# Output projection, LayerNorm and routing of three of four tiles moved into the mixers of a two-layer decoder trunk

## The chip, the core and the metric

One core of a Trainium2 chip runs the whole kernel. Its engines are PE (TensorE, matrix products; PEld is its weight load), DVE (VectorE), ACT (ScalarE), POOL (GpSimd) and SP (SyncE, which issues most transfers). The metric is the time of one execution on the device in microseconds (us). Each engine works through its own queue in order; an instruction that waits holds up all that stands behind it on its engine.

## The reference, cut to what matters

Two layers over 512 positions of 1024 features in float32, 16 experts of width 512, two of which a position uses.

```python
for l in range(2):
    mix = even_mixer(...) if l % 2 == 0 else odd_mixer(...)       # attention, ends in "@ w_o[l]"
    x = layer_norm(ALPHA * x + mix, ln_g[l, 0], ln_b[l, 0])       # LN1
    ffn = routed_moe(x, router_w, router_b, w_gate[l], w_up[l], w_down[l])
    x = layer_norm(ALPHA * x + ffn, ln_g[l, 1], ln_b[l, 1])       # LN2
...
def routed_moe(x, router_w, router_b, ...):
    aff = sigmoid(x @ router_w); sel = aff + router_b
    # best group of 4 experts by the sum of its two best; then the two best experts in it
    # gates: the two aff of the chosen experts, divided by their sum
    for e in range(16):
        h = silu(x @ w_gate[e]) * (x @ w_up[e])
        y = y + gates[:, e:e + 1] * (h @ w_down[e])
```

## The kernel before

The 512 positions are four tiles of 128. Every weight chunk of 1 MB (128 x 2048) is split on the core into a high part (ACT's cast `wh`, L184) and a low part (`wl`, L185, mostly on DVE, some on Pool), and every product is three matmuls (L197 wh by high, L198 wl by high, L199 wh by low). A tile scheduler orders the instructions of each engine; the strings `EVEN_ORDER`, `ODD_ORDER` and `ROUTE_ORDER` give the order in which the program offers the stages to it.

A mixer ends in attention over query tiles: a0 to a3 in layer 0 (span 0 to about 206 us), c0 to c3 in layer 1 (602 to about 820). One such tile is scores (L322, L323), maximum and bias on DVE (L342), exponential on ACT (L356), a multiplication by the reciprocal (`p`, L364, DVE or Pool), transposes (L372), ACT's copies `pT` (L375) and value matmuls (L378), and a split of the result into `XH` and `XL`. `o0` and `o1` are out_proj0, the half of the output projection that needs only the other mixer's heads. When all tiles are done, `out_proj` follows: for each tile `tile_y` (24 projection matmuls, the add into `xr` with L569, bn_stats L570, transposes L574, copy `yT` L576 and logits L578) and `tile_ln` (rsqrt in eight small DVE steps, the logits `u` L584 and L585, ACT's Sigmoid L586 and Identity L587, and the affine by `lnt`: L254 multiplies, L255 adds; `LN1_DVE` says how many of the 1024 columns DVE takes, the rest is Pool's). Then `choose` (L416 to L452) picks the experts of some tiles, `slots` gives each chosen row a slot of the first expert in a one-hot `oh` (L477), and `first_rows` multiplies by it to collect expert 0's rows in PSUM (L488).

`moe` runs the 16 experts: gate and up products (`ps_s`), silu times up, down product (`ps_a`), about 17.7 us an expert. Expert 0's rows come from first_rows, split into `m`; those of the others from an indirect gather (L1089, Pool) of the copy `x1d` in memory, by the index `idx` that `after_slots` makes with eight one-hot matmuls on `R` (L504); a second set of eight (L526, on `og`) gives the gates by slot. `AHEAD` lists the first sixteen chunks in the order in which SP is to load them; each waits for the buffer that it goes into. At the end of a layer, LN2 runs tile by tile: add with a running sum on DVE (L1228), Square on ACT (L1236), Pool and DVE sharing the rest (L1246 to L1256), while layer 1's first weights, the latents' (128 x 968 chunks), are split on Pool.

## Time and profile before

| | us |
|---|---|
| median of 3 runs (1188.57 to 1193.22) | 1191.38 |
| the profiled execution | 1197.56 |
| its span in the trace | 1195.7 |
| PE busy | 1098.3 (92%) |
| DVE, ACT, POOL busy | 935.3, 763.3, 263.2 |

The profile shows one execution, so sums made from its rows are set against 1197.56 and not against the median. Starts are in us from the start of the span. Matmuls overlap, so the time of one in a row (0.39 for a 128x512 matmul) is longer than the distance to the next; the distance is the pace.

### The profile page before, as it was taken

What the parts mean: (1) busy time and instruction counts of PE and PEld (TensorE: products, weight loads), DVE (VectorE), ACT (ScalarE), POOL (GpSimd) and SP (SyncE); (2) the same over time, 40 slices, a digit from 0 to 9 for tenths busy, and PEclk for the clock granted to TensorE, in tenths of its full rate; (3) what the DMA queues carried; (4) which work ended last, traced back from release to release, by engine and by line L of the source; (5) the groups of instructions that cost most, each with busy time, mean ns of one, the idle gap of its engine ahead of it and who ended that gap; (6) DMA issues with size and microseconds to landing.
All of it is one profiled execution on the core that took longest, in us unless ns stands there. A gap on an engine that the chain in (4) does not pass through costs nothing.

```text
span 1195.7 us, 16655 instructions
## 1 busy us (share of the span) xinstructions
PE 1098.3 (92%) x5739; PEld 816.4 (68%) x5739; DVE 935.3 (78%) x1866; ACT 763.3 (64%) x1229; POOL 263.2 (22%) x223
## 2 busy tenths in 40 slices
PE   6999999979999999997599889999799999999972
PEld 5886777867777777776277665777677777777751
DVE  3646746597999999995866999865879999999957
ACT  3557556225888888885435744754268888888852
POOL 2001240251111141102612133003411112311023
PEclk9999999988999999998699999999789999999986
DMA  8313423679899997996512211335699999989952
GB/s 206 116 36 78 83 55 141 246 278 309 295 362 348 353 334 252 365 370 218 163 27 71 71 36 36 106 106 194 247 292 288 368 338 354 329 263 369 370 193 107
DMA packets 139613, 262.25 MB, mean 219 GB/s; under 512 B 11831, under 2 KB 28247, under 8 KB 139520
## 3 DMA queue, kind: packets, MB, share of 16 engines
q1 hardware_dynamic: 129232, 234.62, 57.1%
...
q8 instruction: 47, 0.77, 0.3%
q14 instruction: 46, 0.38, 0.1%
...
## 4 chain that ended last, share of the span: by engine, by line
PE 80%; DVE 10%; ACT 5%; issue 2%; POOL 2%; DMA 1%; SPq 0%; DVEq 0%; ACTq 0%; POOLq 0%
PE ps_a L198 11%; PE ps_a L199 11%; PE ps_a L197 11%; PE ps_s L197 10%; PE ps_s L198 10%; PE ps_s L199 9%; PE ps_o L378 4%; PE ps_t L372 3%; DVE wl L185 2%; ACT wh L184 2%; PE ps_t L1100 2%; PE ps_s L322 1%; POOL wl L185 1%; PE ps_s L323 1%; PE ps_s L578 1%
## 5 line engine op out<-in xcount | busy, mean ns | idle before, releaser
L185 DVE TENSOR_TENSOR wl<-wraw,wh 128x1024 fp32r<-128x1024 f32 (+1 forms) x418 | 500.2, 1222 | 92.8 <-ACT wh L184 82.2
L184 ACT CAST wh<-wraw 128x1024 fp32r<-128x1024 f32 (+3 forms) x436 | 445.8, 1039 | 151.3 <-PE ps_s L199 67.0
L197 PE MATMUL ps_s<-wh,m 128*96 128x512 f32 (+1 forms) x528 | 209.2, 396 | 1.7 <-ACT m L202 1.7
L198 PE MATMUL ps_s<-wl,m 128*96 128x512 f32 (+1 forms) x528 | 206.9, 392 | 0.0
L199 PE MATMUL ps_s<-wh,m 128*96 128x512 f32 (+1 forms) x528 | 205.7, 389 | 0.4 <-DVE m L203 0.4
L198 PE MATMUL ps_a<-wl,hH 128*96 128x512 f32 x256 | 102.4, 400 | 10.4 <-POOL wl L185 10.4
L199 PEld LDWEIGHTS ps_s<-wh,m 128*96 128x96 f32 x528 | 86.7, 164 | 35.8 <-DVE m L203 1.3
L197 PEld LDWEIGHTS ps_s<-wh,m 128*96 128x96 f32 x528 | 87.2, 165 | 34.9 <-ACT m L202 2.1
L198 PEld LDWEIGHTS ps_s<-wl,m 128*96 128x96 f32 x528 | 86.9, 165 | 32.1 <-issue 0.2
L197 PE MATMUL ps_a<-wh,hH 128*96 128x512 f32 x256 | 103.1, 403 | 3.4 <-ACT hH L202 3.4
L199 PE MATMUL ps_a<-wh,hL 128*96 128x512 f32 x256 | 101.4, 396 | 1.3 <-DVE hL L203 1.3
L197 PE MATMUL ps_a<-wh,XH 128*128 128x512 f32 (+2 forms) x224 | 88.6, 395 | 2.6 <-ACT wh L184 1.5
L1089 POOL DMA_INDIRECT m<-x1d,idx x30 | 32.6, 1087 | 257.5 <-PE ps_t L1100 218.6
L199 PE MATMUL ps_a<-wh,XL 128*128 128x512 f32 (+2 forms) x224 | 88.1, 393 | 0.4 <-DVE XL L203 0.4
L1164 POOL DMA_INDIRECT yd<-m,idx x30 | 48.6, 1621 | 179.4 <-ACT m L1163 178.7
L198 PE MATMUL ps_a<-wl,XH 128*128 128x512 f32 (+2 forms) x224 | 87.5, 391 | 0.0
L197 PE MATMUL ps_a<-XH,wh 128*128 128x512 f32 x160 | 65.1, 407 | 0.0
L199 PE MATMUL ps_a<-XH,wl 128*128 128x512 f32 x160 | 64.7, 404 | 0.3 <-DVE wl L185 0.3
L198 PE MATMUL ps_a<-XL,wh 128*128 128x512 f32 x160 | 64.9, 406 | 0.0
L375 ACT COPY pT<-ps_t 128x512 f32<-128x512 f32 (+2 forms) x88 | 43.6, 518 | 31.8 <-PE ps_t L372 28.3
L356 ACT ACTIVATE p<-p,nm 128x256 f32<-128x256 f32 (+3 forms) x96 | 50.7, 530 | 18.4 <-DVE nm L349 9.3
L198 PEld LDWEIGHTS ps_a<-wl,hH 128*96 128x96 f32 x256 | 41.7, 163 | 27.0 <-POOL wl L185 11.8
...
## 6 DMA issues: line engine op xcount, KB each, us to landing
...
```

The source lines that it names most:

```text
L184: first(A.copy(hv, w))
L185: first(eng.tensor_tensor(out=lv, in0=w, in1=hv.bitcast(F32), op=ALU.subtract))
L197: T.matmul(o, lh, rh, start=first, stop=False)
L198: T.matmul(o, lh, rl, start=False, stop=False)
L199: T.matmul(o, ll, rh, start=False, stop=last)
L356: A.activation(out=pt[h], in_=(pt if bias else Sp)[h], func=AF.Exp, bias=nm[:, h:h + 1], scale=(slopes[0][h] if slopes else 1.0), accum_ou ...
L372: T.transpose(tp[h][:, j * 128:(j + 1) * 128], pt[h][:, j * 128:(j + 1) * 128], ident)
L375: A.copy(d_, s_)
L378: T.matmul(O[h * 64:(h + 1) * 64, c0:c0 + 128], vcols(j, h), pT[h][:, j * 128:(j + 1) * 128], start=(j == 0), stop=(j == nb - 1))
L1089: G.indirect_dma_start(out=xg_of[e], out_offset=None, in_=x1d[:, :], in_offset=bass.IndirectOffsetOnAxis(ap=idx[:CAP, e:e + 1], axis=0), b ...
L1100: T.transpose(p[:, k * CAP:(k + 1) * CAP], xg[:, (c * 4 + k) * 128:(c * 4 + k + 1) * 128], ident[:CAP, :CAP])
L1164: G.indirect_dma_start(out=yd[:, :], out_offset=bass.IndirectOffsetOnAxis(ap=idx[:CAP, e:e + 1], axis=0), in_=yos[e % 2], in_offset=None, ...
```

## The change

The output projection's second half, LN1 and the choice of tiles 0 to 2 are now stages inside the mixers' order strings (class `OutProj`: `S` loads, `y` projects and normalizes a tile, `x` applies the affine and writes the tile out, `h2` chooses for tiles 0 and 1). Tile 2's choice and affine and all of tile 3 stand in `all_routed`, behind the mixer. The mean comes from a sum taken with the add, the variance from ACT's Square instead of bn_stats; the logits are copied out of PSUM. The affine of tiles 2 and 3 is DVE's for all 1024 columns, that of tiles 0 and 1 Pool's as before. `R` now holds index and gate side by side in float32, so eight one-hot matmuls replace two sets of eight. The splits of the first two gate chunks and of expert 0's rows are kept in program order behind the one-hot of tile 3 (`issue_after(oh.ins)`). What only the end needs (`oht`, the flag) is made in expert 4. The value matmuls take the second head first. Chunk 7 is loaded last of the sixteen, into another buffer. Both halves of the latents' weights are loaded early instead of one.

```diff
-AHEAD = (2, 3, 4, 0, 1, 5, 6, 8, 9, 10, 12, 13, 7, 14, 11, 15)
-LN1_DVE = (0, 0, 0, 256)
+AHEAD = (2, 3, 4, 0, 1, 5, 6, 8, 9, 10, 12, 13, 14, 11, 15, 7)
+LN1_DVE = (0, 0, 1024, 1024)
-EVEN_ORDER = "a0 a1 a2 a3 o0 o1"
-ODD_ORDER = "d0 q0 d1 q1 R0 d2 d3 r0 r1 t1 t2 t3 c0 c1 o0 o1 c2 c3"
-ROUTE_ORDER = "y0 l0 y1 l1 y2 l2 y3 l3 r02 r23 r34"
+EVEN_ORDER = "a0 o0 a1 o1 S0 y0 x0 a2 y1 x1 h2 a3 y2"
+ODD_ORDER = "d0 q0 d1 q1 R0 d2 d3 r0 r1 t1 t2 t3 c0 c1 o0 o1 S0 c2 y0 x0 y1 x1 h2 c3 y2"
...
         for j in range(nb):
-            for h in range(2):
+            for h in (1, 0):
...
-        R = sm.tile([128, NT * 2, NE], F16, name="R", bufs=1)
-        V.tensor_tensor(out=R, in0=Of, in1=recc.rearrange("p t c -> p (t c)").unsqueeze(2).to_broadcast([128, 8, NE]), op=ALU.mult)
+        R = sm.tile([128, NT * 2, 2, NE], F32, name="R", bufs=1)
+        V.tensor_tensor(out=R[:, :, 0, :], in0=Of, in1=recc.rearrange("p t c -> p (t c)").unsqueeze(2).to_broadcast([128, 8, NE]),
+                        op=ALU.mult)
+        weights()
+        V.tensor_tensor(out=R[:, :, 1, :], in0=Of, in1=gates.rearrange("p t c -> p (t c)").unsqueeze(2).to_broadcast([128, 8, NE]),
+                        op=ALU.mult)
         sp = ps_s()
         for j in range(NT * 2):
-            oh = sm.tile([128, CAP], F16, name="oh", bufs=4)
-            V.tensor_scalar(oh, slot1, pos[:, j:j + 1], None, op0=ALU.is_equal)
-            T.matmul(sp[:CAP, 0:NE], oh, R[:, j, :], start=(j == 0), stop=(j == NT * 2 - 1))
+            eq = sm.tile([128, CAP], F32, name="eq")
+            V.tensor_scalar(eq, slot1, pos[:, j:j + 1], None, op0=ALU.is_equal)
+            T.matmul(sp[:CAP, 0:2 * NE], eq, R[:, j].rearrange("p c e -> p (c e)"), start=(j == 0), stop=(j == NT * 2 - 1))
         V.tensor_scalar(idx[:CAP], sp[:CAP, 0:NE], OOB, None, op0=ALU.add)
+        A.activation(out=gslot[:CAP], in_=sp[:CAP, NE:2 * NE], func=AF.Copy, scale=1.0 / ALPHA)
...
-        sg = ps_t()
-        for j in range(NT * 2):
-            eq = sm.tile([128, CAP], F32, name="eq")
-            V.tensor_scalar(eq, slot1, pos[:, j:j + 1], None, op0=ALU.is_equal)
-            T.matmul(sg[:CAP, 0:NE], eq, og[:, j, :], start=(j == 0), stop=(j == NT * 2 - 1))
-        A.activation(out=gslot[:CAP], in_=sg[:CAP, 0:NE], func=AF.Copy, scale=1.0 / ALPHA)
...
+        def y(self, i, room):
             for c in range(2):
                 ys = xr[i][:, c * 512:(c + 1) * 512]
-                V.tensor_tensor(out=ys, in0=ys, in1=half_proj(rows[c], oH, oL, g, i), op=ALU.add)
-                V.bn_stats(sts[i][:, c, :], ys)
-                if main:
+                V.tensor_tensor_reduce(out=ys, in0=half_proj(self.rows[c], self.oH, self.oL, self.g, i), in1=ys, scale=1.0,
+                                       scalar=(self.ls[:, i, 0:1] if c else 0.0), op0=ALU.add, op1=ALU.add,
+                                       accum_out=self.ls[:, i, c:c + 1])
-                    yT = work.tile([128, 512], F32, name="yT", tag="sg", bufs=2)
+                    yT = room()
                     A.copy(yT, p)
                     for k in range(4):
-                        T.matmul(lgs[:, c, i, :], yT[:, k * 128:(k + 1) * 128], rwg[:, c * 4 + k, :],
+                        T.matmul(p[:, 0:NE], yT[:, k * 128:(k + 1) * 128], self.rwg[:, c * 4 + k, :],
                                  start=(k == 0), stop=(k == 3))
+                    V.tensor_copy(self.lg[:, i, c, :], p[:, 0:NE])
+        def ln(self, i, room):
+            ls = self.ls[:, i]
+            V.tensor_scalar(ls[:, 2:3], ls[:, 1:2], -1.0 / (D * 32), None, op0=ALU.mult)
+            sq = room().bitcast(BF16)
+            A.activation(out=sq, in_=xr[i], func=AF.Square, bias=ls[:, 2:3], scale=1.0 / 32, accum_out=ls[:, 4:5])
+            rs = rsqrt(ls[:, 4:5], LN_EPS, 1)
+            nm = sm.tile([128, 1], F32, name="nmr", bufs=4)
+            V.scalar_tensor_tensor(out=nm, in0=ls[:, 2:3], scalar=32.0, in1=rs, op0=ALU.mult, op1=ALU.mult)
+            A.activation(out=xr[i], in_=xr[i], func=AF.Identity, scale=rs, bias=nm)
+        def x1(self, i):
+            affine(xr[i], self.gb, self.bb, LN1_DVE[i])
...
+        room = lambda: work.tile([128, 512], F32, name="yT", tag="sg", bufs=2)
+        n = NT - 1
+        out.y(n, room)
+        choose(n - 1, n)
+        out.ln(n, room)
+        out.x1(n - 1)
+        ps2 = [ps_o(), ps_s()]
+        slots(out.sl, oh0, 0, n)
+        first_rows(ps2, oh0, 0, n - 1)
+        first_rows(ps2, oh0, n - 1, n)
+        choose(n, NT)
+        out.x1(n)
+        oh = slots(out.sl, oh0, n, NT)
+        first_rows(ps2, oh0, n, NT)
+        return out.sl, ps2, oht, oh
...
-                t = xo.tile([128, 2048], F32, name="wraw3", tag=dict(e=eH, E=eL, l=lL, x=lH)[t])
+                t = xo.tile([128, 2048], F32, name="wraw3", tag=dict(e=eH, E=eL, l=eL, x=lH)[t])
...
-        g0 = [ksplit(load("g", 0, c), 2) for c in range(2)]
         m1 = xo.tile([128, 2, D], F32, name="m1", tag=eH)
-        m2 = xo.tile([128, 2, D], F32R, name="m2", tag=eL)
+        m2 = xo.tile([128, 2, D], F32R, name="m2", tag=lL)
         xgs, yos = [m1[:CAP, j, :] for j in range(2)], []
         gH, gL = (m2[:, j, 0:KD * CAP].rearrange("p (k t) -> p k t", k=KD) for j in range(2))
-        for c in range(2):
-            put_rows(c, ps2[c])
-        after_slots(sl, oht, flag)
+        with tc.issue_after(oh.ins):
+            in_order[0] = True
+            g0 = [ksplit(load("g", 0, 0), 2)]
+            for c in range(2):
+                put_rows(c, ps2[c])
+            g0.append(ksplit(load("g", 0, 1), 2))
+            in_order[0] = False
+        after_slots(sl)
...
+            if e == 4:
+                with tc.issue_after(act_op[0].ins):
+                    for_the_end(sl, oht, flag)
...
-    layer(0, even_mixer(), x1d0, yd0, lambda: early.append(latent_load(0, True)), lambda i: None)
+    layer(0, even_mixer(), x1d0, yd0, lambda: early.extend(latent_load(kh, True) for kh in range(2)), lambda i: None)
```

PE at the first gate of layer 0, before: the two blocks of tile 3's first_rows (`oh`), four of the eight index matmuls (`R`), a transpose, and the first gate matmuls (`m` is expert 0's rows).

```order
L488 MATMUL ps_o<-oh_2287,xr_131 128x96 x4
L488 MATMUL ps_s<-oh_2287,xr_131 128x96 x4
L504 LDWEIGHTS oh
L504 MATMUL ps_s<-R,oh 96x16
L504 LDWEIGHTS oh
L504 MATMUL ps_s<-R,oh 96x16
L504 LDWEIGHTS oh
L504 MATMUL ps_s<-R,oh 96x16
L504 LDWEIGHTS oh
L504 MATMUL ps_s<-R,oh 96x16
L511 MATMUL ps_t<-ident,eq 96x128
L197 MATMUL ps_s<-wh,m_2806 96x512
```

PE at the same place now:

```order
L488 MATMUL ps_o<-oh_2570,xr_131 128x96 x4
L488 MATMUL ps_s<-oh_2570,xr_131 128x96 x4
L508 MATMUL ps_s<-R,eq 96x32 x2
L196 MATMUL ps_s<-wh,m_2784 96x512
L508 MATMUL ps_s<-R,eq 96x32 x2
L197 MATMUL ps_s<-wl,m_2784 96x512
L508 MATMUL ps_s<-R,eq 96x32 x2
L198 MATMUL ps_s<-wh,m_2784 96x512
```

In both the first index matmuls stand ahead of the first gate matmul; now `R` is the tile that also holds the gates.

DVE behind the one-hot of tile 3 in layer 0, before (`m`: the low part of expert 0's rows; `gt` and `a` lead to the gates):

```order
L477 TENSOR_TENSOR oh_2287<-slot_117,sl 128x96
L497 TENSOR_TENSOR pt<-O,sl 128x128
L510 TENSOR_SCALAR eq<-slot_117,sl 128x96
L499 TENSOR_REDUCE pos<-pt 128x8
L503 TENSOR_SCALAR oh<-slot_117,pos 128x96 x4
L457 TENSOR_TENSOR gt<-O,aff 128x128
L203 TENSOR_TENSOR m_2806<-ps_o,m_2806 128x384
L503 TENSOR_SCALAR oh<-slot_117,pos 128x96
L203 TENSOR_TENSOR m_2806<-ps_s,m_2806 128x384
```

DVE at the same place now, from the split of expert 0's rows on (in the row ahead of these stand two `wl` of the first gate chunk):

```order
L202 TENSOR_TENSOR m_2784<-ps_s,m_2784 128x384
L184 TENSOR_TENSOR wl<-wraw_2759,wh 128x1024 x2
L495 TENSOR_TENSOR pt<-O,sl 128x128
L497 TENSOR_REDUCE pos<-pt 128x8
L457 TENSOR_TENSOR gt<-O,aff 128x128
L507 TENSOR_SCALAR eq<-slot_117,pos 128x96
L459 TENSOR_REDUCE a_2813<-gt 128x8
L507 TENSOR_SCALAR eq<-slot_117,pos 128x96
L461 TENSOR_TENSOR as__2815<-a_2813 128x4
L462 RECIPROCAL as__2815<-as__2815 128x4
L463 TENSOR_TENSOR gates<-a_2813,as__2815 128x8
L502 TENSOR_TENSOR R<-O,gates 128x8x16
```

Between the one-hot and `R` there stand now four low halves, and the steps of the gates that came later.

PE at the end of c3 in layer 1, before (`ps_a` are projection matmuls, `p` to `pT` the softmax):

```order
L372 MATMUL ps_t<-ident,p 128x128 x8
L199 MATMUL ps_a<-wh,XL_6958 128x512
L197 MATMUL ps_a<-wh,XH_6956 128x512
L198 MATMUL ps_a<-wl,XH_6956 128x512
L378 MATMUL ps_o<-pT,vc 64x128
L199 MATMUL ps_a<-wh,XL_6958 128x512
L197 MATMUL ps_a<-wh,XH_6956 128x512
L378 MATMUL ps_o<-pT,vc 64x128 x7
L198 MATMUL ps_a<-wl,XH_6956 128x512
L199 MATMUL ps_a<-wh,XL_6958 128x512
L197 MATMUL ps_a<-wh,XH_6956 128x512
L198 MATMUL ps_a<-wl,XH_6956 128x512
```

PE at the same place now:

```order
L371 MATMUL ps_t<-ident,p 128x128 x8
L321 MATMUL ps_s<-kc,qs 128x512
L322 MATMUL ps_s<-kc,qs 128x512
L378 MATMUL ps_o<-pT,vc 64x128 x8
L371 MATMUL ps_t<-ident,p 128x128 x8
L378 MATMUL ps_o<-pT,vc 64x128 x8
L371 MATMUL ps_t<-ident,p 128x128 x11
L378 MATMUL ps_o<-pT,vc 64x128 x8
L371 MATMUL ps_t<-ident,p 128x128 x5
L571 MATMUL ps_t<-ident,xr_5507 128x128 x4
L378 MATMUL ps_o<-pT,vc 64x128 x8
L575 MATMUL ps_t<-rwgb,yT 128x16 x4
```

The projection matmuls that stood between transposes and value matmuls are gone from there.

POOL at the end of layer 0, before (128x968 `wl` are the latents' low halves, the rest LN2's):

```order
L185 TENSOR_TENSOR wl<-wraw,wh 128x968 x2
L1246 TENSOR_SCALAR xr_5533<-xr_5533,ls 128x256
L1247 TENSOR_TENSOR xr_5533<-xr_5533,lnt 128x256
L1246 TENSOR_SCALAR xr_5533<-xr_5533,ls 128x256
L1247 TENSOR_TENSOR xr_5533<-xr_5533,lnt 128x256
L185 TENSOR_TENSOR wl<-wraw,wh 128x968
L1255 TENSOR_TENSOR xr_5533<-xr_5533,lnt 128x256 x2
L1246 TENSOR_SCALAR xr_5536<-xr_5536,ls 128x256
L1247 TENSOR_TENSOR xr_5536<-xr_5536,lnt 128x256
L185 TENSOR_TENSOR wl<-wraw,wh 128x968
```

POOL at the same place now:

```order
L184 TENSOR_TENSOR wl<-wraw,wh 128x968 x4
L1294 TENSOR_SCALAR xr_5504<-xr_5504,ls 128x256
L1295 TENSOR_TENSOR xr_5504<-xr_5504,lnt 128x256
L1294 TENSOR_SCALAR xr_5504<-xr_5504,ls 128x256
L1295 TENSOR_TENSOR xr_5504<-xr_5504,lnt 128x256
L1303 TENSOR_TENSOR xr_5504<-xr_5504,lnt 128x256 x2
L1294 TENSOR_SCALAR xr_5507<-xr_5507,ls 128x256
```

All four low halves stand ahead of LN2's steps.

## Rows read from the trace of the kernel before

**Rows 1.** The page's first part: busy time of each engine, share of the span, instructions.

```profile
PE 1098.3 (92%) x5739; PEld 816.4 (68%) x5739; DVE 935.3 (78%) x1866; ACT 763.3 (64%) x1229; POOL 263.2 (22%) x223
```

**Rows 2.** Windows of the core: from and to, length, then for PE, PEld, DVE, ACT and POOL the busy us (and instructions), the granted clock of PE as a share of full speed, the DMA engines' busy share and GB/s.

```profile
256.00:276.00 20.00, 14.91 (x103) 13.98 (x102) 16.50 (x71) 3.48 (x6) 7.70 (x7) 0.79 0.94 323
570.00:600.00 30.00, 15.87 (x57) 10.14 (x56) 24.86 (x57) 11.84 (x19) 18.31 (x14) 0.66 0.47 139
780.00:820.00 40.00, 39.88 (x261) 29.33 (x260) 24.07 (x76) 20.29 (x48) 0.00 (x0) 1.00 0.23 80
850.00:872.00 22.00, 18.08 (x111) 17.00 (x110) 17.98 (x73) 4.68 (x8) 9.47 (x8) 0.68 0.86 292
```

**Rows 3.** Timeline of PE in the projection of layer 0's tiles, and two of layer 1: start, us, engine, line, operation, and in brackets the idle time before it and what ended it.

```profile
246.36 0.66 PE L574 MATMUL ps_t<-ident,xr 128*128 128x128 f32 x4 [2.90 <-DVE xr L569]
...
253.02 0.63 PE L198 MATMUL ps_a<-wl,XH 128*128 128x512 f32 x1
253.44 0.63 PE L199 MATMUL ps_a<-wh,XL 128*128 128x512 f32 x1
...
254.15 0.39 PE L198 MATMUL ps_a<-wl,XH 128*128 128x512 f32 x1
254.38 0.39 PE L199 MATMUL ps_a<-wh,XL 128*128 128x512 f32 x1
...
840.62 0.74 PE L574 MATMUL ps_t<-ident,xr 128*128 128x128 f32 x4 [3.01 <-DVE xr L569]
...
847.95 0.40 PE L198 MATMUL ps_a<-wl,XH 128*128 128x512 f32 x1
```

**Rows 4.** Timeline of POOL (the affine of a tile) and of DVE (the first steps of a choice at the same time, and the first step of a later choice).

```profile
238.73 2.38 POOL L254 TENSOR_TENSOR xr<-xr,lnt 128x1024 f32<-128x1024 f32 x1 [1.79 <-ACT xr L587]
...
239.42 1.73 DVE L416 TENSOR_TENSOR sel<-aff,rb 128x32 f32<-128x32 f32 x1
241.19 2.42 DVE L420 TENSOR_TENSOR pr<-sel 128x16 f32<-128x16 f32 x1
...
267.42 0.16 DVE L416 TENSOR_TENSOR sel<-aff,rb 128x16 f32<-128x16 f32 x1
```

**Rows 5.** Timeline of PE from the last projection matmul of layer 0 to the gate, and expert 1's first rows.

```profile
255.52 0.40 PE L199 MATMUL ps_a<-wh,XL 128*128 128x512 f32 x1
...
272.30 1.99 PE L488 MATMUL ps_o<-oh,xr 128*128 128x96 f32 x8 [0.63 <-DVE oh L477]
274.09 1.91 PE L488 MATMUL ps_s<-oh,xr 128*128 128x96 f32 x8
...
276.19 0.77 PE L197 MATMUL ps_s<-wh,m 128*96 128x512 f32 x1
...
277.19 0.63 PE L199 MATMUL ps_s<-wh,m 128*96 128x512 f32 x1
...
291.45 0.47 PE L197 MATMUL ps_s<-wh,m 128*96 128x512 f32 x1 [0.85 <-ACT m L202]
```

**Rows 6.** Timeline of PE in layer 1: the last projection matmul and the first gate matmul.

```profile
850.02 0.40 PE L199 MATMUL ps_a<-wh,XL 128*128 128x512 f32 x1
...
871.36 0.77 PE L197 MATMUL ps_s<-wh,m 128*96 128x512 f32 x1
```

**Rows 7.** Groups of instructions by line and shape, whole span: count, busy us, mean ns of one, idle time before them.

```profile
L185 DVE TENSOR_TENSOR wl<-wraw,wh 128x1024 fp32r<-128x1024 f32 x408 | 492.5, 1232 | 89.5 <-ACT wh L184 79.0 <-DMA wraw<-in_moe_w_up_dram 1.7 <-DMA wraw<-in_moe_w_gate_dram 0.2
...
L375 ACT COPY pT<-ps_t 128x512 f32<-128x512 f32 x48 | 27.2, 587 | 22.4 <-PE ps_t L372 19.5 <-PE ps_s L383 2.5
...
L356 ACT ACTIVATE p<-p,nm 128x512 f32<-128x512 f32 x16 | 11.6, 723 | 4.8 <-DVE nm L351 3.2 <-DVE nm L349 1.5
...
L1236 ACT ACTIVATE sq<-xr,ls 128x1024 f32<-128x1024 f32 x8 | 9.2, 1148 | 5.4 <-DVE ls L1234 5.2
...
L526 PE MATMUL ps_t<-og,eq 128*96 128x16 f32 x32 | 3.8, 216 | 0.0
```

**Rows 8.** Timeline of ACT in layer 1: Identity, table load, Sigmoid.

```profile
821.38 1.25 ACT L587 ACTIVATE xr<-xr,nmr,rs_o 128x1024 f32<-128x1024 f32 x1
822.66 1.28 ACT L586 ACT_TABLE_LOAD   x1
824.06 0.21 ACT L586 ACTIVATE aff<-u 128x16 f32<-128x16 f32 x1
```

**Rows 9.** Timeline of DVE in layer 0: the end of tile 3's choice (`M`), its one-hot, and the step after it.

```profile
270.04 0.17 DVE L452 TENSOR_TENSOR M<-O 128x16 f16<-128x16 f16 x1
...
271.90 0.26 DVE L477 TENSOR_TENSOR oh<-slot,sl 128x96 f32<-128x96 f16 x1
272.07 0.28 DVE L497 TENSOR_TENSOR pt<-O,sl 128x128 f32<-128x128 f16 x1
```

**Rows 10.** Timeline of the end of layer 0: POOL's low half of the latents' weights; DVE's LN2 steps beside it (the first of them without such a neighbour); PE's first transposes for layer 1.

```profile
583.45 2.22 POOL L185 TENSOR_TENSOR wl<-wraw,wh 128x968 fp32r<-128x968 f32 x1
...
580.63 1.02 DVE L1248 SCALAR_TENSOR_TENSOR xr<-xr,ls,lnt 128x768 f32<-128x768 f32 x1 [0.26 <-ACT sq L1236]
...
583.54 2.15 DVE L227 SCALAR_TENSOR_TENSOR rs_p<-rs_c 128x2 f32<-128x2 f32 x1
...
590.44 4.38 DVE L1248 SCALAR_TENSOR_TENSOR xr<-xr,ls,lnt 128x768 f32<-128x768 f32 x2
...
587.92 0.69 PE L275 MATMUL ps_t<-ident,xr 128*128 128x128 f32 x2 [9.03 <-POOL xr L1255]
```

More of the change, by code (lines that the diff above doesn't have):

```diff
@@ L572, in tile_y @@
+                if self.main:
                     p = ps_t()
@@ L594, in out_proj @@
-        if not main:
-            for i in range(NT):
-                tile_y(i)
-                tile_ln(i)
-            return
-        ps2 = None
-        for f, *n in ROUTE_ORDER.split():
-            i = int(n[0])
-            if f == "y":
-                tile_y(i)
-            elif f == "l":
-                tile_ln(i)
-            else:
-                j = int(n[1])
-                if i == 0:
-                    ps2 = [ps_o(), ps_s()]
-                choose(i, j)
-                slots(sl, oh0, i, j)
-                first_rows(ps2, oh0, i, j)
@@ L812, in even_mixer @@
             last = attn_b((2, 3), q1, ks, split_tile, True)
+            room = lambda: work.tile([128, 512], F32, name="yT", tag="pT", bufs=3)
             for f, n in EVEN_ORDER.split():
+                n = int(n)
                 if f == "a":
-                    last(int(n))
-                else:
-                    out_proj0(wo_src, oH, oL, 0, (int(n),))
-            return wo_src, oH, oL, 1
+                    last(n)
+                elif f == "o":
+                    out_proj0(wo_src, oH, oL, 0, (n,))
+                elif f == "S":
+                    out = OutProj(0, wo_src, oH, oL, 1, x1d0, yd0, True)
+                elif f == "y":
+                    out.y(n, room)
+                    out.ln(n, room)
+                elif f == "x":
+                    out.x1(n)
+                else:
+                    choose(0, n)
+            return out
     def latent_load(kh, push=False):
@@ L1014, in wo_src @@
                 return lambda v: [(v, wo[g * 512:(g + 1) * 512, c * 512:(c + 1) * 512].rearrange("(k p) c -> p k c", p=128))]
+            room = lambda: work.tile([128, 512], F32, name="yT", tag="pT", bufs=3)
             oH = None
@@ L1035, in odd_mixer, with moe @@
                     out_proj0(wo_src, oH, oL, 1, (n,))
-            return wo_src, oH, oL, 0
-    def moe(l, mo, sl, ps2, oht, x1d, yd, flag, following, finish):
+                elif f == "S":
+                    out = OutProj(1, wo_src, oH, oL, 0, x1d1, yd1, main)
+                elif f == "y":
+                    out.y(n, room)
+                    out.ln(n, room)
+                elif f == "x":
+                    out.x1(n)
+                elif main:
+                    choose(0, n)
+            if not main:
+                out.y(NT - 1, room)
+                out.ln(NT - 1, room)
+                for n in (NT - 2, NT - 1):
+                    out.x1(n)
+            return out
+    def moe(l, mo, sl, ps2, oht, oh, x1d, yd, flag, following, finish):
         last = NE - 1
@@ L1159, in scatter @@
             if not yos:
-                m3 = xo.tile([128, 2, D], F32, name="m3", tag=lL)
+                m3 = xo.tile([128, 2, D], F32, name="m3", tag=eL)
                 yos.extend(m3[:CAP, j, :] for j in range(2))
```

80 lines of the change are left out of this document (38 added, 42 removed).

## The prediction

> **What bounds the kernel now.** I read the engines' shares first: PE is busy for 1098 of 1195.7 us [rows 1], so time is won only where PE idles or runs at the lower of its two clocks. The windows then show where that is: 780 to 820 (attention c2 and c3) is full at full clock, while the routing stages and the end of layer 0 lose both ways; PE is busy 14.9 of 20 us at a granted clock of 0.79 in 256 to 276, 18.1 of 22 at 0.68 in 850 to 872, and 15.9 of 30 at 0.66 in 570 to 600 [rows 2]. In a routing stage two things happen. First PE stops while DVE is late with the add of a tile: 2.90 us in layer 0, 3.01 us in layer 1, and after that it runs at half clock (a 128x512 matmul every 0.43 us instead of 0.23, so 1.2 instead of 2.4 GHz) for 7.5 us in layer 0 (246.36 to 253.9) and about as long (840.62 to 847.9) in layer 1 [rows 3]. DVE is late since its small two-input operations wait for Pool's 128x1024 affine: 1.73 and 2.42 us where the same step takes 0.16 later (267.42) [rows 4]. Second, from the last projection matmul (T0) to the first gate matmul of the experts a chain through PE, DVE and ACT runs: in layer 0 from the last matmul's end (255.52 + 0.40) to 276.19, 20.3 us [rows 5], and in layer 1 from 850.42 to 871.36, 20.9 us [rows 6].
>
> **Part 1, up to T0, layer 0.** The stall (2.9) and half of the 7.5 us at half clock (about 3.5) go, 6.4 us, if the mixer hides the new work. By the order, tiles y1 to y3 give PE 72 projection matmuls of 0.23 us, 16.8 us, from the last scores of a3 to T0, which is enough to cover that tile's softmax. New gaps: the affines of tiles 0 and 1 stay on Pool and can hold up DVE's softmax steps as in [rows 4], one such wait (1.7 to 2.4 us) a tile, part of it covered. Bounds of what comes back: 0.9 us (nearly all covered) and 6.4 (all of it again); I take 3.7, the two waits less a little cover. Net **-2.7**.
>
> **Part 2, up to T0, layer 1.** The same goes (3.0 + 3.5 = 6.5). But here the order uses up the work that filled c3: before, 24 projection matmuls stand between c3's transposes and value matmuls; now y1 and y2 are through before them, and y3 needs c3's result. What is left is the softmax chain itself, with ACT as its limit: between c3's scores and its result ACT now has eight exponentials (0.72, and with the read of its sum about 0.9 each), eight copies of 0.59, two more copies or casts of 0.59, a 128x1024 Square of 1.15, an Identity of 1.25 and three table loads of 1.28: 7.3 + 4.7 + 1.2 + 1.15 + 1.25 + 3.84 = 19.4 us [rows 7, 8], and it starts some 3 us after the last matmul of y1 and waits about 2 us for DVE: 25 us. PE's own work in that stretch is 16 score matmuls and 24 projections at 0.23 and some 80 small ones at about 0.1, 18 us. Stall **+7** (4 to 10, by how much the scores' steps overlap). While it lasts PE works in bursts, and the 2.9 us pause of [rows 3] already cost 7.5 us at half clock; y3's 24 matmuls take 10.3 us at half clock instead of 5.6. I take **+3** (0 to 5). Net of this part: -6.5 + 7 + 3 = **+3.5**.
>
> **Part 3, T0 to the gate.** Only tile 3 is left to choose, which sounds short, but its steps form one chain: add with sum 0.7, transposes 0.6 (0.66 in [rows 3]), copy 0.59, Square with its read 1.3 [rows 7], eight small steps of rsqrt at about 0.2 (such steps show 0.16 to 0.28 in [rows 4, 9]) = 1.6, logits and bias 0.5, Identity 1.25, two whole affine operations on DVE at 1.23 [rows 7] = 2.5, the choice 2.8 (267.42 to 270.21) and slots to one-hot 0.8, as rows of the stage before show [rows 4, 9], together 12.6. Tile 2's choice, slots and 288-wide one-hot (3.7 us of DVE) and one or both of its affine operations lie on the same engine; the waits for Square and Identity hide about half of them. T_oh, the end of the one-hot, comes at T0 + 15 (14 to 16.5); before it was 272.16 - 255.92 = 16.2. So the moved work gains about 1.2 us. Then comes the price. Before, the gate began 4.0 us after T_oh, when PE was through with tile 3's first_rows, 1.99 and 1.91 us at half clock [rows 5]. Now the four low halves of the first gate weights are tied behind the one-hot (4 x 1.23 = 4.9; before, they stood ahead of it), then two subtractions of 0.56, and only then the ten small steps to R (0.28 for pt [rows 9], the narrow ones less; I put 2.4 for all); and PE's queue has the first two matmuls with R ahead of the first gate matmul. Nothing can pass them, so the gate starts at T_oh + 8.3 + 0.2. T0 + 23.5 against 20.3 and 20.9: **+3** and **+2.5** (bounds 22 to 25, so +1 to +5 in either layer). Meanwhile PE idles for 4.5 us or more, longer than the 2.9 us pause, and starts the gate at half clock; that pause cost 3.6 us [rows 3], the present start loses less, as PE comes to it from first_rows without a pause (its matmuls are at 0.63 only to about 277.7 [rows 5]); I count 0.7. **+2.9** a layer (0 to 3.6).
>
> **Part 4, after the gate.** The second set of one-hot matmuls goes (3.8 us for both layers, so 1.9 [rows 7]), and the first set becomes float32 like it, twice the passes (+0.9). The 0.85 us wait for the gathered rows of expert 1 [rows 5] goes, as their index is ready earlier against the gate. **-1.85** a layer. oht and the flag move to expert 4, where they cost what they did. The loads: seven chunks of 1 MB that were loaded while the tiles were projected now wait for tile 2's copy and Square. The last of the sixteen is now issued when DVE is through with the one-hot's followers, about 3 us ahead of the gate, and is used 20 us after it. I cost it at 0.
>
> **Part 5, the end of layer 0.** Two of the four low halves of the latents' weights now run on Pool between its LN steps, and hold up DVE and with it PE: an rsqrt step of 0.16 takes 2.15 behind one (583.45), two steps of 1.02 take 4.38 behind the other, and PE stands still for 9.03 us before [rows 10]. With all four ahead of the LN steps, 2.0 + 2.3 go: **-4** (-4.4, or 0 if ACT's casts are late and the four sit in front of the LN steps). The reversed heads change which copy the first value matmul waits for, by one copy at most each way, under other work: 0 (within 1).
>
> **Sum.** Layer 0: -2.7 + 3 + 2.9 - 1.85 = +1.35. Layer 1: +3.5 + 2.5 + 2.9 - 1.85 = +7.05. End of layer 0: -4. Total **+4.4 us**: 1202.0 against the profiled 1197.56; the median of the runs shown is 1191.38, 6.2 us lower, and against it the same sum gives **1195.8 us**. A change of under 0.5% (6 us) can't be told from none in measurements of this kernel, so this counts as no change.
>
> **A rule of the Trainium skill that speaks against the change.** The rows of layer 1 show an Identity that ends at 822.63, a table load of 1.28 us and the sigmoid at 824.06 [rows 8]: 1.4 us in all for a switch of functions.
> The Trainium skill, "ScalarE: Activation LUTs", section "What ACT_TABLE_LOAD costs", adds a drain of about 1.38 us to each switch, 2.66 us in all; by it the sum would be about 1200. The trace speaks against it, with 0.12 us behind the load and none ahead of it.
>
> **Rivals.**
> Slower: the hole in c3. The mechanism is part 2 at its upper end: ACT's chain starts late because the first exponential stands behind tile 1's Square and a table load, DVE's p multiplications wait on Pool's affines of tile 1, and PE stays at half clock from the first hole through y3. Then the stall is 10 and the clock 5, 5 more than in my sum, and with the gate at T0 + 25 in both layers 1.5 more in each: 1203.8. It decides as soon as PE's idle time between the last projection of y2 and the first of y3 is over 7 us. For it: no other work of PE is ready there. Against it: DVE and ACT are busy for only 24.1 and 20.3 of the 40 us of 780 to 820 now [rows 2].
> Faster: the wait behind R is hidden and the hole is small. If DVE gets two of the low halves done while PE is at first_rows and the chain to R runs in PE's shadow, the gate starts when it did (T0 + 20.3, so -3.2 and -2.5, and no added half clock, -2.9 a layer; -11.5), which gives 1184.3; with c3's stall at 4, 1181.3. For it: DVE is relieved of Pool's locks. Against: the order of PE and DVE, which allows nothing to pass.
> A switch of functions costs ACT twice what its load shows, 1.28 us more at each of the three loads in c3 [rows 8]: 3.8 more, 1199.6. The Trainium skill's drain (above) is such a rule.
> The early experts wait for weights, as seven loads start 30 us later: a wait of up to 3.2 us for each late chunk (1 MB at the 323 GB/s of 256 to 276 [rows 2]); with two late ones a layer, 1209.
>
> **How the numbers follow.** Forecast as worked out (1187 to 1200): 0.38. Faster rival: 0.28. Hole in c3: 0.25. Table switch: 0.03. Late weights: 0.06. Faster by over 0.5% (under 1185.4): 0.28; within: 0.37; slower (over 1197.3): 0.35, the last two with the forecast's upper edge and the table rival on the slow side. The range for 8 in 10 reaches to both larger rivals: 1180 to 1209; the forecast's own is 1187 to 1200.
>
> **What would show it.** Right: PE rows with idle time behind DVE's R ahead of the first gate matmul in both layers, 4 us or more, and half-clock matmuls behind it; in layer 1 PE idle of about 7 us among the last transposes and value matmuls of c3; no 2.15 us rsqrt step at the end of layer 0, and its first transposes about 2 us sooner after the last expert. Wrong: a first gate matmul less than 21 us after the last projection, c3 without holes, or PE waiting for DMA in experts 0 to 3.

## The result and the profile after

| | before | after |
|---|---|---|
| median (4 runs each, side by side) | 1191.22 | **1207.43** (1199.92 to 1209.26) |
| profiled execution, its span | 1197.56, 1195.7 | 1206.48, 1204.7 |

The ratio is 1.0134, with a 95% interval of 1.0088 to 1.0181: slower by 1.3%, where the forecast had no change. It lies inside the range for 8 in 10 (1180 to 1209), close to its end, and outside the forecast's own (1187 to 1200). The profiled execution of before lies above all its timed ones; a second one, of an unchanged copy (last of the second group below), came to 1187.32 with a span of 1185.5. I set the stretches of after beside both. A stretch goes from mark to mark: start, last projection matmul of layer 0 (T0), first gate matmul, first silu, last silu, T0 of layer 1, gate, first silu, last silu, end (differences of starts in the timelines of PE and ACT).

| us | to T0 | gate | 1st silu | last silu | T0, L1 | gate | 1st silu | last silu | end |
|---|---|---|---|---|---|---|---|---|---|
| before | 255.5 | 20.7 | 9.9 | 260.2 | 303.7 | 21.3 | 10.9 | 260.2 | 53.2 |
| before, 2nd | 255.1 | 21.0 | 9.6 | 260.2 | 299.3 | 21.9 | 11.0 | 260.2 | 47.4 |
| after | 252.5 | 25.3 | 12.6 | 265.0 | 299.7 | 25.7 | 11.5 | 265.0 | 47.4 |

The experts' stretch is the steadiest (260.2 four times), and it is 4.8 us longer in either layer: the change's largest loss, where the prediction had a gain. The handover, from T0 to the gate, costs 3.8 to 4.6 us a layer more, where 2.5 to 3 were forecast.

After, the page's first part (busy us, share, instructions) answers to [rows 1]:

```profile
PE 1089.8 (90%) x5719; PEld 811.3 (67%) x5719; DVE 923.9 (77%) x1866; ACT 779.5 (65%) x1251; POOL 253.0 (21%) x215
```

PE has 8.5 us less work than in [rows 1] and a span 9 us longer: what was lost is waiting. After, the timeline of PE at the handover of layer 0, then of layer 1, answers to [rows 5] and [rows 6]:

```profile
277.13 0.82 PE L508 MATMUL ps_s<-R,eq 128*96 128x32 f32 x4 [6.21 <-DVE R L502]
277.77 0.72 PE L196 MATMUL ps_s<-wh,m 128*96 128x512 f32 x1
...
284.47 0.63 PE L198 MATMUL ps_s<-wh,m 128*96 128x512 f32 x1
285.21 0.39 PE L197 MATMUL ps_s<-wl,m 128*96 128x512 f32 x1
...
880.20 0.82 PE L508 MATMUL ps_s<-R,eq 128*96 128x32 f32 x4 [6.21 <-DVE R L502]
880.83 0.72 PE L196 MATMUL ps_s<-wh,m 128*96 128x512 f32 x1
```

PE stands for 6.21 us until R is there, and then works at half clock to about 284.9 (0.43 us from matmul to matmul, 0.23 after). What DVE does meanwhile in layer 0, from the end of tile 3's one-hot (268.85) on:

```profile
268.76 2.35 DVE L184 TENSOR_TENSOR wl<-wraw,wh 128x1024 fp32r<-128x1024 f32 x2
...
272.42 2.36 DVE L184 TENSOR_TENSOR wl<-wraw,wh 128x1024 fp32r<-128x1024 f32 x2 [0.37 <-ACT wh L183]
274.69 0.28 DVE L495 TENSOR_TENSOR pt<-O,sl 128x128 f32<-128x128 f16 x1
...
276.70 0.29 DVE L502 TENSOR_TENSOR R<-O,gates 128x128 f32<-128x128 f16 x1
```

The four low halves, with the two subtractions between them, take 6.0 us; the ten steps to R take 2.3. The part that the prediction missed comes 30 us later. After, PE at the second half of expert 1's up product, and ACT beside it:

```profile
304.82 0.82 PE L1138 MATMUL ps_t<-ident,m 96*128 96x96 f32 x8
306.83 0.48 PE L196 MATMUL ps_s<-wh,m 128*96 128x512 f32 x1 [1.18 <-ACT wh L183]
...
308.09 0.47 PE L197 MATMUL ps_s<-wl,m 128*96 128x512 f32 x1 [0.78 <-DVE wl L184]
...
310.06 0.63 PE L197 MATMUL ps_s<-wl,m 128*96 128x512 f32 x1
```

```profile
302.41 0.47 ACT L201 CAST hH<-ps_t 128x384 fp32r<-128x384 f32 x1
305.36 0.48 ACT L201 CAST m<-ps_t 128x384 fp32r<-128x384 f32 x1 [2.48 <-PE ps_t L1138]
305.73 3.89 ACT L183 CAST wh<-wraw 128x1024 fp32r<-128x1024 f32 x4
```

The weights' casts (305.73) stand on ACT behind the cast of expert 2's rows, which waits 2.48 us for PE's transposes; PE reaches the up product and waits for those very casts, 1.18 and 0.78 us, and works at half clock from 308.9 to 312.2 (0.43 us a matmul, some 1.5 us more than at full clock). The chunk is the last of `AHEAD` now, issued by SP at 274.81, 31 us ahead of its casts. If SP's queue moves its loads in the order of their issue, the bytes that it has moved cover this one by about 282.5, an estimate from the trace's packets: the wait is not for the DMA, but for a place in ACT's order.

After, PE at c3 in layer 1 and at the latents' transposes, which answers to [rows 10]:

```profile
832.82 1.51 PE L371 MATMUL ps_t<-ident,p 128*128 128x128 f32 x6 [4.86 <-DVE rm L445]
...
839.68 0.55 PE L378 MATMUL ps_o<-pT,vc 128*64 128x128 f32 x6 [0.73 <-ACT pT L374]
```

```profile
597.85 0.48 PE L274 MATMUL ps_t<-ident,xr 128*128 128x128 f32 x1 [5.37 <-POOL xr L1303]
...
604.29 1.09 PE L274 MATMUL ps_t<-ident,xr 128*128 128x128 f32 x4 [2.40 <-POOL xr L1295]
```

The hole in c3 is there, 4.86 and 0.73 us, and the waits of the transposes fell from 9.03 and 3.25 to 5.37 and 2.40.

### The profile page after: what moved, and what is told of

It is laid out like the page before. It is cut to its first block, busy times and chain, and to the rows that moved or that the text cites. A ratio compares the mean times of both kernels' runs of the same rounds, so it can differ in the third digit from the quotient of the medians.

```text
span 1204.7 us, 16567 instructions
## 1 busy us (share of the span) xinstructions
PE 1089.8 (90%) x5719; PEld 811.3 (67%) x5719; DVE 923.9 (77%) x1866; ACT 779.5 (65%) x1251; POOL 253.0 (21%) x215
## 5 line engine op out<-in xcount | busy, mean ns | idle before, releaser
L198 PEld LDWEIGHTS ps_s<-wh,m 128*96 128x96 f32 x528 | 87.1, 165 | 37.5 <-DVE m L202 2.3
L1204 POOL DMA_INDIRECT yd<-m,idx x30 | 53.5, 1782 | 188.9 <-ACT m L1203 187.9
```

The lines of the kernel that those rows point to most:

```text
L198: T.matmul(o, ll, rh, start=False, stop=last)
L1204: G.indirect_dma_start(out=yd[:, :], out_offset=bass.IndirectOffsetOnAxis(ap=idx[:CAP, e:e + 1], axis=0), in_=yos[e % 2], in_offset=None, ...
```

## The experiments, first group: the changed kernel with one thing undone

Medians and ratios are against runs of the kernel before on the same chip (1190.63, then 1189.91, then 1190.73, one for each group); the changed kernel itself ran beside the four of 1191.22. The ratios are not the quotients of these medians (for e2 that would be 1.0070, its ratio is 1.0087). Differences to the changed kernel in us, below, are between medians of different rounds, and its own interval is wide: the ratios say how firm they are. The theory: the handover waits for R (A), and the late casts of expert 1 (C) are a cost of their own. The rival (B): the handover is one chain, and a wait that is taken away comes back as another.

**e1_gates_first.** The slot work is issued behind twelve gate matmuls.

```diff
-        after_slots(sl)
-        for e in (1, 2):
-            gather(e)
         for e in range(NE):
-            g = up("g", e, None if e else g0)
+            g = up("g", e, None if e else g0, 1, None if e else lambda: after_slots(sl))
+            if e == 0:
+                for j in (1, 2):
+                    gather(j)
```

> The changed kernel, except that the slot work (the eight one-hot matmuls of 32 columns, that wait for R) is issued behind the first 12 matmuls of expert 0's gate; same work. Theory A (the loss is the wait for R at each handover, 6.21 us of idle TensorE in either layer, and the half clock that follows it): the idle in front of the first gate matmul falls from 6.2 to 1 to 3 us, from the last tile's one-hot matmuls to the gate it takes 19 to 21 us instead of 24.9, and the time falls by 7 to 11 us, to 1197 to 1200 (ratio to the kernel before 1.005 to 1.007). Theory B (the slots come later now, so the gathers do, and expert 1's rows take over as the wait): the idle moves to the transposes of expert 1's rows, and the time stays within 3 us of 1207 (1.011 to 1.016). Theory C (the loss is the late loads of expert 1's up weights): the same as B at the gate, the 1.2 + 0.8 us wait of expert 1's second up chunk remains, and the time falls by less than 5 us.

1205.4, ratio 1.0147 (1.0112 to 1.0182). T0 to gate fell to 19.8 and 18.0 us, but the experts' stretch grew to 277.6 and 274.6. PE in layer 0:

```profile
281.86 0.82 PE L508 MATMUL ps_s<-R,eq 128*96 128x32 f32 x4 [4.18 <-DVE R L502]
...
294.48 0.74 PE L1138 MATMUL ps_t<-ident,m 96*128 96x96 f32 x3 [2.89 <-DMA m<-x1d,idx]
```

B: the twelve matmuls run early, then PE waits for R all the same, and the gathered rows are late. From T0 to the last silu it takes 306.1 and 301.3 us, 302.9 and 302.2 after: PE's order wasn't the cause; DVE's chain to R is.

**e2_old_load_order.** Loads, rooms and untied low halves of before; the slot work is left as changed.

```diff
-AHEAD = (2, 3, 4, 0, 1, 5, 6, 8, 9, 10, 12, 13, 14, 11, 15, 7)
+AHEAD = (2, 3, 4, 0, 1, 5, 6, 8, 9, 10, 12, 13, 7, 14, 11, 15)
-                t = xo.tile([128, 2048], F32, name="wraw3", tag=dict(e=eH, E=eL, l=eL, x=lH)[t])
+                t = xo.tile([128, 2048], F32, name="wraw3", tag=dict(e=eH, E=eL, l=lL, x=lH)[t])
...
-        m2 = xo.tile([128, 2, D], F32R, name="m2", tag=lL)
+        m2 = xo.tile([128, 2, D], F32R, name="m2", tag=eL)
...
-        with tc.issue_after(oh.ins):
...
+        g0 = [ksplit(load("g", 0, c), 2) for c in range(2)]
```

> The changed kernel with the loads and rooms of before: the ahead list of before, the seventh load in the fourth room, expert rows in the second room, and expert 0's low halves no longer tied behind the one-hot; the slot work is still in front of the gate. Theory A (the wait for R is the loss): the idle in front of the gate remains at 5 to 6.2 us a layer and the time falls by no more than 3 us (1204 to 1208, ratio 1.011 to 1.014). Theory C (the loss is the late casts of expert 1's second up chunk, 1.18 + 0.78 us of wait and some 1.5 us of half clock behind it, a layer): that wait is gone, expert 3's rows come 3 to 5 us earlier against the gate in both layers, and the time falls by 6 to 9 us (1198 to 1201, ratio 1.006 to 1.008). If the tie itself holds R back, the idle in front of the gate falls as well, to under 3 us, and the time to 1192 to 1197.

1198.95, ratio 1.0087 (1.0058 to 1.0116): 8.5 us under the changed kernel by the medians, 0.0047 by the ratios, whose intervals overlap. The trace shows C: the silus of experts 1 and 2 are 17.6 us apart again (23.0 and 21.4 after), and ACT has the second chunk's casts in their place:

```profile
301.30 0.60 ACT L1163 ACTIVATE sg<-ps_s 96x512 f32<-96x512 f32 x1
301.79 1.04 ACT L183 CAST wh<-wraw 128x1024 fp32r<-128x1024 f32 x1
303.03 1.05 ACT L183 CAST wh<-wraw 128x1024 fp32r<-128x1024 f32 x1 [0.20 <-PE ps_s L198]
```

Which of the three, the order of the loads, the rooms or the tie, moved the casts is not separated. The experts' stretch is 262.2 and 262.1: the last four steps from silu to silu take 16.5, 18.9, 18.3 and 18.1 us in layer 0 (17.7 each after). The wait for R fell to 3.52 and 2.11 us, so the tie is part of it. But T0 to gate is still 24.2 and 24.4: in layer 0 two of the four low halves now stand ahead of the one-hot, which ends at T0 + 17.5 (16.0 after). Most of the handover's loss remains.

**e3_both_undone.** Both edits.

> Both edits together: the loads and rooms of before, and the slot work behind the first 12 gate matmuls. If A and C both hold and add up: 13 to 19 us under the changed kernel, 1188 to 1194 (ratio 0.997 to 1.003). If each hides the other's wait (B): no better than the better of the two alone, 1197 to 1201.

1203.73, ratio 1.0122 (1.0087 to 1.0156): slower than e2 alone by the medians and above both numbers. With R further back the gathers are, and PE waits for them (4.63 and 4.51 us).

**e4_c3_filled.**

```diff
-ODD_ORDER = "d0 q0 d1 q1 R0 d2 d3 r0 r1 t1 t2 t3 c0 c1 o0 o1 S0 c2 y0 x0 y1 x1 h2 c3 y2"
+ODD_ORDER = "d0 q0 d1 q1 R0 d2 d3 r0 r1 t1 t2 t3 c0 c1 o0 o1 S0 c2 y0 x0 c3 y1 x1 h2 y2"
```

> The changed kernel with the last unit of the second layer's c attention moved ahead of the output projection of tiles 1 and 2, so that the projection's matmuls fill c3's softmax chain. Theory: the hole in front of c3's transposes (TensorE idle 4.86 us, one wait for DVE's choice) goes, and of 26 us in which TensorE worked 19.4 the idle falls by 4 to 6: 1201 to 1204 (ratio 1.009 to 1.011). Rival: the projection, the LN and the choice of tile 2 are then late instead (they stand on DVE behind c3's maxima and scalings), the same idle shows between the last projection and the choice of the last tile, and the time stays at 1205 to 1209.

1203.84, ratio 1.013 (1.0101 to 1.016): 3.6 us under the changed kernel by the medians, level with it by the ratios (1.0134), so no gain is shown. In the profile, which caught the fastest of its six executions, the stretch up to T0 of layer 1 fell by 12.2 us (287.5), and T0 to gate rose by 5.2 (30.9), where tile 2's choice is now late:

```profile
851.49 0.20 PE L469 MATMUL ps_s<-M,tri 128*128 128x48 f16 x1 [4.10 <-DVE M L452]
```

## Second group: two one-hot sets

The theory was now that R waits for the gates (weight product, sums, reciprocal, product on DVE), which one set for index and gates brought in.

**f1_two_sets.** The sets of before, index first:

```diff
-        R = sm.tile([128, NT * 2, 2, NE], F32, name="R", bufs=1)
+        R = sm.tile([128, NT * 2, NE], F16, name="R", bufs=1)
...
+        V.tensor_scalar(idx[:CAP], sp[:CAP, 0:NE], OOB, None, op0=ALU.add)
+        weights()
+        og = sm.tile([128, NT * 2, NE], F32, name="og", tag="gt", bufs=1)
...
```

> The changed kernel with the one-hot sets of before: the eight f16 index matmuls first, the gates' product, its eight f32 one-hots and matmuls and the copy of the gates behind them; loads, rooms and the tie stay as changed. Theory A2 (what holds the first gate matmul is not that the slot work stands in front of it, but that R now needs the gates: weight product, two sums, reciprocal and product on DVE): the wait in front of the first slot matmul falls from 6.2 to 2.5 to 4 us in either layer, from the last projection to the gate it takes 21.5 to 23 us instead of 25.3, expert 1's gather comes as early as before, and the time falls by 4 to 8 us against the changed kernel (1199 to 1203, ratio 1.007 to 1.011). Rival (the four low-half casts in front of it hold it): the wait stays at 5 us or more and the second set costs its 1.9 us a layer besides: 1207 to 1211.

1202.89, ratio 1.0094 (1.0064 to 1.0124), 4.5 us under the changed kernel by the medians, with intervals that overlap. The wait fell only to 4.71 us, between the two numbers, and T0 to gate to 23.2 and 22.9: the tied low halves hold it too. And the gate is not the whole of it: the second set's matmuls stand among the gate's, at half clock, and from gate to first silu it takes 15.8 and 14.6 us (12.6 and 11.5 after). From T0 to the first silu this kernel gains nothing (39.1 and 37.5; 37.9 and 37.2 after).

**f2_two_sets_old_loads.** f1 and e2 together.

> The same two one-hot sets, and the loads, rooms and untied low halves of before as well (those of the second run above, which took 8 us off). If both causes are separate they add up: 12 to 16 us under the changed kernel, 1191 to 1195 (ratio 0.999 to 1.004), with 20.5 to 22 us from the last projection to the gate. If they are one cause seen twice: 1197 to 1200.

**1193.28**, ratio 1.0028 (1.0009 to 1.0046): of the 0.0134 that the change lost, 0.0106 is back, 14.2 us by the medians. This is clear of the intervals of the changed kernel, of f1 (1.0094; what f2 has more are the loads, and both ran on one chip) and of e2 (1.0087; what f2 has more are the two sets): each edit counts where the other is in. By the medians e2's 8.5 and f1's 4.5 nearly add up to it, but the handover shows that they are not separate: to the first silu it takes 32.7 and 30.5 us, 37.2 and 36.6 in e2, and the two sets without the old loads gained nothing there. The wait for the slots is 2.02 us in layer 0 and T0 to gate nearly that of before (21.8 and 20.7):

```profile
271.99 0.21 PE L504 MATMUL ps_s<-R,oh 128*96 128x16 f16 x1 [2.02 <-DVE oh L503]
```

**f3_and_c3_filled.** f2 with e4's order.

> As the one before, with the last c unit ahead of the projection of tiles 1 and 2 (the order that took some 3.6 us off above). If it adds up: 1187 to 1192 (ratio 0.996 to 1.001), that is level with or a little under the kernel before. Rival: since the choice of the last tile but one then ends right at the last projection, the handover of the second layer is longer by as much as the hole was, and it is no faster than the one before it.

1195.42, ratio 1.0031 (1.0008 to 1.0055): the rival. It has 8.7 us less up to T0 of layer 1 and 7.1 more from there to the gate, with the same 4.10 us wait for M. I read the hole in c3 and the wait for the choice as one chain on DVE.

**c0_before_again.** The kernel before.

> The kernel before, unchanged, profiled once more: its only profiled execution (1197.56) lies above all its timed ones (1183 to 1193). If that execution was a chance, a new one lies at 1188 to 1194, and the landmarks of the profile shift by where the clock was granted longer; if the profiler adds some 6 us to this kernel, it lies at 1196 to 1199 again. The ratio is 0.997 to 1.003 in either case.

1189.83, ratio 1.0001 (0.9979 to 1.0023), profiled at 1187.32: the first profiled execution was a chance. The rows differ in waits for Pool's last low half (4.90 and 5.53 us of PE in one, 2.60 and 2.15 in the other).

## Third group: the other parts

**g1_and_flag_early.** f2, with the transposed one-hot and the flag straight behind the slots:

```diff
         after_slots(sl)
+        for_the_end(sl, oht, flag)
...
-            if e == 4:
-                with tc.issue_after(act_op[0].ins):
-                    for_the_end(sl, oht, flag)
```

> The changed kernel with two one-hot sets, the loads, rooms and untied low halves of before (as in the run that came to 1193.28), and the transposed one-hot and the overflow flag back behind the slots instead of at expert 4. Theory: the profile shows expert 4 longer by 0.8 us in every kernel that has them there, and no expert of the kernel before is longer for them; so 1.6 us come off, 1190 to 1192.5 (ratio 1.000 to 1.002). Rival: DVE has no room for their 4 one-hots and the maximum in expert 0, the low halves of expert 1 are late by them, and the time stays at 1193 to 1196.

1194.62, ratio 1.0025 (1.0004 to 1.0046): no gain. Expert 4 fell from 18.5 to 17.7 us, but the experts' stretch is 262.9 and 263.9 as in f2: the last experts take 18.3 in both. Why those do isn't settled.

**g2_ln_on_pool.** g1, with `LN1_DVE = (0, 0, 0, 256)`.

> As the one before, with the LN's weight and bias of tiles 2 and 3 on GpSimd again (LN1_DVE of before): DVE loses four passes of 128 by 1024, some 5 us, between the last projection and the gate, and GpSimd does them. Theory A (DVE's queue sets the handover): from the last projection to the gate it takes 18 to 19.5 us instead of some 21, and the time falls by 2 to 4 us, to 1187 to 1190 (ratio 0.997 to 1.000), which is under the kernel before. Rival (GpSimd's passes hold tile 3's rows back, and with them the gather of expert 1, or slow DVE beside them): the same or up to 5 us slower, with the wait on a DMA in front of expert 1's rows.

1204.66, ratio 1.0121 (1.0084 to 1.0158): 10 us slower, so the affines on DVE are worth that much in this order. POOL and DVE in layer 0 show why, as [rows 4] did:

```profile
249.41 2.35 POOL L253 TENSOR_TENSOR xr<-xr,lnt 128x1024 f32<-128x1024 f32 x1 [6.32 <-ACT xr L598]
251.84 2.36 POOL L254 TENSOR_TENSOR xr<-xr,lnt 128x1024 f32<-128x1024 f32 x1
```

```profile
249.46 2.33 DVE L416 TENSOR_TENSOR sel<-aff,rb 128x16 f32<-128x16 f32 x1 [1.27 <-ACT aff L595]
251.83 0.17 DVE L420 TENSOR_TENSOR pr<-sel 128x8 f32<-128x8 f32 x1
251.91 2.31 DVE L421 TENSOR_TENSOR pr<-sel 128x8 f32<-128x8 f32 x1
```

Two DVE steps of 16 and 8 elements last as long as Pool's two passes of 1024 beside them. T0 to gate became 28.9 and 24.0.

**b1_before_latents.** The kernel before, with one edit:

```diff
-lambda: early.append(latent_load(0, True))
+lambda: early.extend(latent_load(kh, True) for kh in range(2))
```

> The kernel before with one part of the change alone: both halves of the latents' weights loaded and split ahead of the last LN of the first layer. The prediction gave this part 4 us, from the wait of the latents' transposes on GpSimd (9.03 and 3.25 us of idle TensorE): the idle is 5 to 6 and 2.4 us here and the time falls by 3 to 5 us (ratio 0.996 to 0.9975). Rival: the low halves are late somewhere else (the wait is passed to the first d projection), and it is within 1 us of the kernel before (0.999 to 1.001).

1189.41, ratio 0.9979 (0.9957 to 1.0001): the time is unclear. The place is not: the waits of the transposes are 5.38 and 2.40 us (9.27 and 3.25 in the second profile of before), and the stretch up to T0 of layer 1 is 5.6 us under that profile's. Only 2.5 of the 5.6 lie ahead of the first c scores. The other 3.1 lie in the projection of the last tile: behind the same wait of 3.0 us for DVE it takes 6.3 us from the transposes to T0 here, and 9.4 in both profiles of before. The granted clock makes the difference; windows from those transposes to T0, as in [rows 2], of the second profile of before, of this kernel and of the next one (the last figure but two is the clock):

```profile
835.70:845.20 9.50, 9.46 (x36) 7.84 (x36) 6.55 (x23) 4.92 (x7) 1.76 (x1) 0.64 0.29 116
...
837.10:843.50 6.40, 6.38 (x36) 5.29 (x36) 6.15 (x23) 4.39 (x6) 0.58 (x1) 1.00 0.46 183
...
830.90:837.30 6.40, 6.38 (x36) 5.29 (x36) 6.15 (x23) 4.39 (x6) 0.58 (x1) 1.00 0.47 190
```

No edit is there, and why the clock stayed up in two of the four executions is open. From T0 to the gate this execution has 1.6 and 0.8 us more.

**b2_before_heads.** The kernel before, with one edit:

```diff
         for j in range(nb):
-            for h in range(2):
+            for h in (1, 0):
                 T.matmul(O[h * 64:(h + 1) * 64, c0:c0 + 128], vcols(j, h),
```

> The kernel before with the two heads' attention products in reversed order and nothing else. The prediction gave this part 0 (within 1 us): the waits of the d units on the softmax's second half (2.11 and 1.75 us) shift or go, but not what follows them. In the changed kernel the d units are 2.9 us shorter, and if it is the reversed heads that shorten them, the time falls by 2.5 to 3 us here, all of it between the first d and the first c scores (ratio 0.9975 to 0.998).

**1185.83**, ratio 0.9952 (0.9923 to 0.9981): faster than both kernels, 4.9 us under the one before and 1.8% under the changed one (1185.83 / 1207.43). But not where it was expected: against the second profile of before the first c scores come only 1.0 us earlier (744.30 and 745.31), T0 of layer 1 7.9 us (837.2 and 845.1). Of the 6.9 us between, 3.1 are the clock in the last tile's projection, as in b1, and 3.8 lie in the c units (a unit is a pair of heads of one query tile). PE at one c unit, of the second profile of before, then of this kernel:

```profile
804.49 0.43 PE L378 MATMUL ps_o<-pT,vc 128*64 128x128 f32 x2
804.85 0.50 PE L197 MATMUL ps_a<-wh,XH 128*128 128x512 f32 x1
805.19 0.39 PE L198 MATMUL ps_a<-wl,XH 128*128 128x512 f32 x1
805.51 1.09 PE L378 MATMUL ps_o<-pT,vc 128*64 128x128 f32 x14
806.53 1.09 PE L372 MATMUL ps_t<-ident,p 128*128 128x128 f32 x8
```

```profile
805.79 1.09 PE L378 MATMUL ps_o<-pT,vc 128*64 128x128 f32 x16
806.82 1.09 PE L372 MATMUL ps_t<-ident,p 128*128 128x128 f32 x8
```

In program order the first product (two matmuls in the row) needs the first copy of pT only, so it was issued while the second was still being copied, and projections went between: 0.36 + 1.02 us in two pieces, 1.03 in one. Over layer 1 the 320 matmuls stand in 44 pieces that take 28.5 us to whatever comes next, and in 30 that take 22.9 (summed over PE's timeline behind 640 us): 5.6 us, of which 3.7 behind the first c scores, nearly all of the 3.8. The changed kernel has 30 pieces too and 24.3 us. The Trainium skill, "TensorEngine Tiling (Array Packing)", section "Key Properties", has TensorE drain at a change of tiling mode; these products are 64 columns wide among matmuls of 128, and the 0.35 us for one more piece agrees with that, though no row shows in which mode they run, and no run here separates the drain from the pipeline's filling.

## Why the prediction came out as it did

**Part 1**, layer 0 up to T0: -2.7 forecast, -3.0 and -2.6 against the two profiles of before. Right, as a sum.

**Part 3**, T0 to the gate: T0 + 23.5 forecast, 24.9 and 25.3 measured as the forecast counts, from that matmul's end (the table goes from its start): at the upper bound of 25. The one-hot ended at T0 + 16.0 in layer 0, where 15 was forecast, and from there to the gate it took 8.9 us, where 8.5 was. So the mechanism was right, with one thing less: the low halves and the gates stand ahead of R on DVE (e2, f1 and f2), but PE's order, which the prediction named too, is not what costs the time (e1). A wait of "4.5 us or more" was 6.21. From gate to first silu it takes 2.7 to 3.1 us more in layer 0 (2.9 forecast for the half clock) and 0.5 to 0.6 in layer 1. The half clock accounts for that: it lasts 7.1 us from the gate on in layer 0 (1.5 before) and 4.8 in layer 1 (3.6 before), and half of what it lasts longer is 2.8 and 0.6.

**Part 4**, behind the gate, is the step that failed: -1.85 a layer forecast, +4.8 measured, 13.3 us in the two layers, more than the 11.8 that lie between a sum of +4.4 and the 16.2 of the medians. The "I cost it at 0" of the loads looked at when the data come. No wait for them shows, but in ACT's order the last chunk's casts came to stand behind a cast that waits for PE, and PE waited for them (e2: the 17.6 us step is back). The rival with late weights had the place, not the mechanism: no DMA was waited for. The range's end, 1209, is what that rival gave, at a chance of 0.06, so that 1207.43 lies inside is in part luck. The transposed one-hot at expert 4, costed at what it was, added 0.8 us a layer to expert 4; g1 takes that away and gains nothing. The 0.85 us wait at expert 1's rows did not go either: it became two in either layer, about 1.03 and 0.67, for their high and their low part.

**Part 2**, layer 1 up to T0: the hole was there (5.6 us, +7 forecast). With part 5 the stretch was forecast at -0.5 (+3.5 - 4); it measured -4.0 against the first profile of before and +0.4 against the second. But the hole can't be taken by itself: f3 pays again, as a wait for the choice, 7.1 of the 8.7 us saved up to T0, and e4 5.2 of 12.2.

**Part 5**: the latents' -4 was right in the waits, but 2.5 us is what the profile of b1 shows ahead of the c scores, and the time can't tell it from none (-1.3 by the medians, interval -5.1 to +0.1). "The reversed heads" at "0 (within 1)" was wrong; alone they give 4.9 us by the medians (2.3 to 9.2 by the interval). I had weighed which copy is waited for, not into how many pieces PE's order falls. If both gains carry over whole to the changed kernel (2.5 and 4.8 us in the profiles of b1 and b2 up to T0 of layer 1, without the 3.1 of the clock), the interleaving of layer 1 costs some 8 us there, since after and the second profile of before are level in that stretch (+0.4); no run shows that sum by itself. The 3.1 us also touch a premise of parts 1 and 2: that the 2.9 us pause brings the half clock behind it. It did in both profiles of before, and in layer 1 of b1 and b2, behind the same pause, it did not.

The rival of the table switch: after, a load at 825.18 of 1.28 us follows an Identity that ends at 825.16, and the sigmoid starts at 826.48; no drain is to be seen here either.

The rows of after for it, of ACT:

```profile
823.92 1.24 ACT L594 ACTIVATE xr<-xr,nmr,rs_o 128x1024 f32<-128x1024 f32 x1 [0.78 <-DVE nmr L593]
825.18 1.28 ACT L591 ACT_TABLE_LOAD   x1
826.48 0.22 ACT L591 ACTIVATE aff<-u 128x16 f32<-128x16 f32 x1
```
